# Attention scores of a decoder trunk: plain fp32 products against three products of rounded halves

## The chip, the core and the metric

The kernel runs on one core of a Trainium2 chip. The time is that of the device for one execution, in microseconds (us), and the number to be forecast is the median over several executions. PE is the matmul engine (TensorE; PEld is its weight load), DVE is VectorE, ACT is ScalarE, POOL is GpSimd, SP is the engine that issues the DMAs.

## The reference

A trunk of two layers over 256 tokens of width 1024. Layer 0 is a half-step gated FFN, a short convolution, another half-step FFN. Then one shared set of keys and values is made, and layer 1 is an FFN, sparse attention with 16 heads in 4 key groups, and an FFN. The attention has three branches over the same queries: compressed blocks of keys, selected blocks (at 256 tokens: all of them) and a window. What matters here are the three products of queries and keys:

```python
s_c = jnp.einsum('bghqd,bgnd->bghqn', qblk, k_c) * scale + head_bias(rel_c)
...
s_s = jnp.einsum('bghqd,bgqkd->bghqk', qblk, k_sel) * scale + bias_s
...
s_w = jnp.einsum('bghqd,bgkd->bghqk', qblk, k_wb) * scale + head_bias(rel_w)
```

Each is followed by a masked softmax, a product with that branch's values, and a gate; the sum of the three goes through the output weights. Everything is float32.

## The kernel before

The kernel is one long stream of matmuls. All large products are made in the type fp32r, a rounded fp32 that PE takes in one pass: a weight tile is split into a high part (a rounded copy, ACT, line 165, tile wh) and a low part (the rest, DVE, line 182, tile wl), activations likewise (xs, act), and three of the four partial products are summed. Small products, such as the scores, were left in plain fp32; the compiled program makes two matmul instructions of each.

Two places matter.

**The background of the FFN of layer 1** (`ffn_in` with `bg(f)`, f = 0 to 21, from about 500 to 625 us of the span). While PE makes the 22 column groups of the FFN, `bg(f)` is called at the end of group f and puts small steps of the key and value preparation into the engines' queues. `k_trans` (f = 6, 7) transposes the keys on PE and ACT scales them into the tile KT (tag kt). `kc_second` and `kc_norm` (f = 15, 18) make the compressed keys: a product with ones, a root on ACT, a reciprocal on DVE, and two DVE instructions that write the first 16 columns of KT. `c_values` (f = 19) makes the compressed values: POOL copies `a` into a repeated form (`a4`, line 923), and PE multiplies it (line 925).

**The attention stage** (about 700 to 760 us). Its order is written out by hand: the string `ORDER` lists words such as `S_0`, and each word calls a function that puts its instructions into the queues. Each engine executes its queue strictly in that order. The heads are handled in eight pairs j. `QT_g` (`q_trans`) transposes queries on PE into a PSUM bank; `QC_g` (`q_gain`) scales them on ACT into an act tile, which serves pairs 2g and 2g+1. `S_j` (`scores`) makes the scores of pair j in two tiles of two PSUM banks (tag mm, two of them in all): head g2 = 0 in array rows 0 to 63, g2 = 1 in rows 64 to 127, for key columns 288, 224 and 304. `M_j_g2` (`minima`, DVE) adds the bias and takes minima, which frees the PSUM tile; `E` (`exps`, ACT) makes exponentials; `R`, `N` normalise (DVE, POOL), `T`, `H` transpose (PE), `C`, `CH` copy out (ACT, or DVE with a suffix d), `U`, `V` multiply by values (PE), `O`, `P` split the result. `F` is one step of work for later on PE, the second half of the query product (`later_queries`, three matmuls a word), and `WA`, `WD` split the next weights. `GA` to `GD` make the gates. The part of the order around the first scores reads:

```python
qs_0 GT qr_0 qs_1 GC F qr_1 F root exp F F WA_0 recip qn_0 qn_1 QT_0 GA GX QC_0 F S_0 WA_1 WD_0 M_0_1 GE QT_1 M_0_0
E_0_1 E_0_0 QC_1 F F R_0_1 F S_1 F F F GD M_1_1 M_1_0 N_0_1 R_0_0 F S_2 CM_0 F F F F E_1_1 R_1_1 CX_0 N_0_0_d SQ_0
...
```

Of the kernel before, what the change touches and what calls it, by code (L numbers as in the profile page):

```python
# [9 lines left out]
F32 = mybir.dt.float32  # L10
F32R = mybir.dt.float32r
I32 = mybir.dt.int32
AF = mybir.ActivationFunctionType
ALU = mybir.AluOpType
AX = mybir.AxisListType

P = 128
T = 256
# [10 lines left out]
G_FFN1, G_MIX, G_FFN2, G_KV, G_CONV, G_Q, G_K = 0, 16, 32, 48, 56, 80, 81  # L29
# [39 lines left out]
def trunk(ctx, tc, A, out):  # L69
    nc = tc.nc  # L70
    ve, ac, pe, po, sy = nc.vector, nc.scalar, nc.tensor, nc.gpsimd, nc.sync
# [9 lines left out]
    def mk(shape, tag, bufs, dt=F32, pool=None):  # L81
        uid[0] += 1
        return (pool or sb).tile(list(shape), dt, tag=tag, name=f"{tag}_{uid[0]}", bufs=bufs)
# [3 lines left out]
    def one(shape, name, dt=F32):  # L87
        if name not in kept:
            kept[name] = cp.tile(list(shape), dt, tag=name, name=name)
        return kept[name]  # L90
# [5 lines left out]
    def bank(shape=(P, 512)):  # L96
        return mk(shape, "a", 4, pool=ps)

    def bank2():
        return mk([P, 2, 512], "mm", 2, pool=ps)  # L100

    def act(shape=(P, 512), dt=F32R):
        return mk(shape, "act", 22, dt)

    def t2(shape=(P, 512), dt=F32):
        return mk(shape, "t2", 7, dt)

    def t1(shape=(P, T)):
        return mk(shape, "t1", 6)
# [120 lines left out]
    gt = base[:, :G_N]  # L230
# [4 lines left out]
    for n, (lo, hi) in enumerate(zip(FIRST, FIRST[1:])):  # L235
# [3 lines left out]
        for dst in todo:  # L239
            m = P * dst.shape[1]  # L240
# [6 lines left out]
    parts = {(f, g): kt8[:, g[0]:g[-1] + 1, T + f * 2 * P:T + (f + 1) * 2 * P].rearrange("p k (u m) -> p u k m", u=2)  # L247
             for f in range(2) for g in GROUPS}
# [8 lines left out]
    gq = one([P, 1], "gq")  # L257
# [27 lines left out]
    def new_xs():  # L285
        return [mk([P, 512], "xs", 8, F32R) for _ in range(8)]
# [453 lines left out]


    xs = new_xs()
    xk_a = mk([P, 4, 512], "kt", 1, F32R)
    xkv = [xk_a[:, k] for k in range(4)] + [t2(dt=F32R) for _ in range(4)]
    nm = Norm([(xkv, G_KV), (xs, G_FFN1 + 8)])
    out_proj(hid, 0.5, nm)
# [72 lines left out]
    for tt in range(2):  # L819
        for x in range(2):  # L820
            src = oc[tt][:, x * 256:(x + 1) * 256].rearrange("p (a d) -> p a d", d=64)
            ac.activation(cn[tt][x], src[:, :, None, :].to_broadcast([P, 4, 2, 64]), AF.Copy, scale=rc[:, tt:tt + 1])

    KT = mk([P, 2, 528], "kt", 1)
    raw = [mk([P, 16, 64], t, NBUF) for t in ("wh", "wl")]
    for r in raw:
        po.memset(r.rearrange("p i m -> p (i m)"), 0.0)
# [2 lines left out]
    def k_trans(tt):  # L830
        pb = bank()
        for q in range(4):
            pe.transpose(pb[:, q * P:(q + 1) * P], kns[tt][:, q * P:(q + 1) * P], ident)
        for b in range(2):
            c0 = KC[b] + tt * P
            ac.activation(KT[:, :, c0:c0 + P], pb[:, b * 256:(b + 1) * 256].rearrange("p (g t) -> p g t", g=2), AF.Copy,
                          scale=gt[:, G_K + 1 + b:G_K + 2 + b])

    def c_trans(tt, x):
        pb = bank([P, 4, P])  # L840
# [65 lines left out]
    def kc_norm(pc, q):  # L906

        pb = bank()
        pe.matmul(pb[:, :64], ones, q, start=True, stop=True)
        r = t1([P, 64])  # L910
        ac.activation(r, pb[:, :64], AF.Sqrt, scale=1.0 / P, bias=epst)
        ve.reciprocal(r, r)
        for g2 in range(2):
            z = slice(g2 * 64, g2 * 64 + 64)
            v, i = [x[z, :64].rearrange("p (a g n) -> p a g n", a=2, g=2)[:, :, g2] for x in (pc, r)]
            ve.scalar_tensor_tensor(out=KT[z, :, :16], in0=v, scalar=gt[z, G_K:G_K + 1], in1=i, op0=ALU.mult, op1=ALU.mult)

    def c_values(a):

# [12 lines left out]
    def bg(f):  # L932
# [8 lines left out]
        elif f in (2, 3, 4, 5):  # L941
            c_trans((f - 2) % 2, (f - 2) // 2)
        elif f in (6, 7):
            k_trans(f - 6)
        elif f == 8:
            po.tensor_tensor(out=both, in0=ident[:, :64], in1=ident[:, 64:], op=ALU.add)
            po.tensor_tensor(out=both48, in0=ident[:96, :48], in1=ident[:96, 48:96], op=ALU.add)
        elif f == 9:
            kv["rk"] = rh_split(0)
        elif f == W1AT[0]:  # L950
            kv["ak"] = c_hidden(kv["rk"])
        elif f == 12:
            kv["ak"] = c_total(kv["ak"])
            kv["rv"] = rh_split(1)
            W.limit = NBUF
        elif f == 13:
            kv["ak"] = c_gelu(*kv["ak"])
        elif f == W1AT[1]:
            kv["av"] = c_hidden(kv["rv"])
            kv["kc"] = kc_second(kv["ak"])  # L960
        elif f == 16:
            kv["av"] = c_total(kv["av"])
        elif f == 17:
            kv["av"] = c_gelu(*kv["av"])
        elif f == 18:
            kc_norm(*kv["kc"])
        elif f == 19:
            c_values(kv["av"])
# [16 lines left out]
    qt, ct, oT, wo, wo_banks, X = {}, {}, [], [], [], {}  # L985
# [56 lines left out]
                pe.transpose(pb[:, a, tt * P:(tt + 1) * P], X["q", q, tt][:, c0 + a * P:c0 + a * P + P], ident)  # L1042

    def q_gain(g):
        q = act([P, 2, T], F32)
        ac.activation(q, X.pop(("qt", g)), AF.Copy, scale=gq)
        for a in range(2):
            qt[2 * g + a] = q[:, a]

    def later_queries():  # L1050

# [52 lines left out]
    def scores(j):  # L1104

        s = [bank2().rearrange("p a b -> p (a b)") for _ in range(2)]
        kt = KT[:, j // 4]
        k0 = kt[:, :512].rearrange("p (a b) -> p a b", a=2)[:, :, :144]
        for c0, c1, tt, k in ((0, 288, 0, k0), (288, 512, 1, kt[:, :224]), (512, 816, 1, kt[:, 224:])):
            for g2 in range(2):  # L1110
                rows = slice(g2 * 64, g2 * 64 + 64)
                pe.matmul(s[g2][:, c0:c1], qt[j][rows, tt * P:(tt + 1) * P], k[rows], start=True, stop=True)  # L1112
        X["s", j, 0], X["s", j, 1] = s

    def minima(j, g2):
# [135 lines left out]
    def wo_part(c, part):  # L1251
# [11 lines left out]
        "exp": lambda: ac.preload_act_table_set("natural_log_exp_and_others"), "qn": lambda tt: q_normed(0, tt),  # L1263
        "SQ": lambda tt: q_square(1, tt), "RD": lambda tt: q_reduce(1, tt),
        "NW": lambda: q_newton(1), "QM": lambda tt: q_normed(1, tt), "QT": q_trans, "QC": q_gain,
        "F": lambda: next(lq), "GT": g_sum, "GC": g_copy, "GA": g_total, "GX": g_trans, "GE": g_exp, "GD": g_out,
        "S": scores, "M": minima, "E": exps, "R": recip,
        "N": lambda j, g, e="": normed(j, g, ve if e else po), "T": trans, "H": trans_hi,
        "C": lambda j, g, e="": copied(("t", j, g), mk([P, 2, T], "xs", 8), copy[e]),
# [126 lines left out]
```

## Time and profile before

| what | value |
|---|---|
| median of 3 runs | 967.46 us (967.12 to 968.42) |
| span of the profiled execution | 965.5 us, 1.96 us under that median (what lies around the span) |
| PE busy | 960.8 us, 100% of the span |
| DVE busy | 730.5 us, 76% |
| ACT busy | 573.9 us, 59% |
| POOL busy | 127.8 us, 13% |
| granted PE clock | 1.000 |
| line 1112 (scores) | 96 matmul instructions, from 706.8 to 744.7 us |

The profile is one execution. Times in its views are microseconds from the start of the span. A row of the timeline gives start, duration, engine, line, operation, output and inputs, and in brackets the idle time just before it with what ended it. A row of the chain of work that ended last gives start, length and the work; there the length is the step to the next link, so a run of n matmuls divided by n is the pace at which they start. The ends of matmuls are modelled, so a PE that is busy 100% still has waits in it; the chain and the starts show them.

### The profile page before, as it was taken

The page shows a single profiled execution, that of the slowest core. Times are in us where ns is not written, and L with a number is a line of the kernel's source. Part 1 is how long each engine was busy: PE and PEld are TensorE (multiplying, and loading weights), DVE is VectorE, ACT ScalarE, POOL GpSimd, SP SyncE. Part 2 cuts the span into 40 slices and gives each one's busy share as a digit, 9 for nine tenths or more (in the row PEclk, how much of TensorE's full clock was granted, in tenths as well). Part 3 has the DMA queues.
Part 4 walks back from the last instruction along what each step waited for, and adds up shares of the span by engine and source line. Part 5 has one row for each costly group of instructions (what it writes and reads, how often), then busy time and mean ns, then how long its engine had stood idle before and what let it go on. Part 6 is the DMA issues. An engine that isn't in the chain of part 4 may idle for free.

```text
span 965.5 us, 14561 instructions
## 1 busy us (share of the span) xinstructions
PE 960.8 (100%) x5620; PEld 843.3 (87%) x5620; DVE 730.5 (76%) x1158; ACT 573.9 (59%) x977; POOL 127.8 (13%) x207
## 2 busy tenths in 40 slices
PE   9999999999999999999999999999999999999998
PEld 8888888888888888888888888888877888888888
DVE  6898875678898787865749988766579798878643
ACT  7666653555466665644656677645589776566430
POOL 2000000154420100001111012100138110000000
PEclk9999999999999999999999999999999999999999
DMA  8665554555546875545645567545511256555541
GB/s 307 215 222 183 208 177 175 202 177 198 189 170 221 234 235 179 199 159 206 217 134 173 178 218 258 174 175 191 198 57 40 93 200 236 176 182 208 183 153 60
DMA packets 28577, 177.61 MB, mean 184 GB/s; under 512 B 3115, under 2 KB 6699, under 8 KB 7900
## 3 DMA queue, kind: packets, MB, share of 16 engines
q1 hardware_dynamic: 28508, 176.69, 53.1%
q8 instruction: 44, 0.72, 0.3%
q14 instruction: 25, 0.20, 0.1%
HBM read 175.59 MB, written 1.08 MB: 183 GB/s over the span
## 4 chain that ended last, share of the span: by engine, by line
PE 96%; DVE 3%; ACT 1%; issue 0%; ACTq 0%
PE mm L425 25%; PE a L498 17%; PE mm L430 13%; PE mm L353 9%; PE a L504 9%; PE mm L358 5%; PE a L353 3%; PE a L358 2%; PE mm L1112 1%; PE mm L574 1%; PE a L761 1%; PE a L763 1%; PE a L762 1%; PE a L1189 1%; DVE wl L182 1%; PE a L1157 1%
## 5 line engine op out<-in xcount | busy, mean ns | idle before, releaser
L182 DVE TENSOR_TENSOR wl<-ws,wh 128x1024 fp32r<-128x1024 f32 x318 | 391.8, 1248 | 51.9 <-ACT wh L165 33.8
L165 ACT CAST wh<-ws 128x1024 fp32r<-128x1024 f32 x318 | 327.0, 1045 | 40.9 <-PE a L498 12.1
L425 PE MATMUL mm<-xs,wh 128*128 128x512 f32 x1088 | 255.5, 391 | 0.3 <-DVE t L368 0.3
L425 PEld LDWEIGHTS mm<-xs,wh 128*128 128x128 f32 x1088 | 201.4, 188 | 40.8 <-DVE t L368 0.8
L498 PE MATMUL a<-act,wh 128*128 128x512 f32 x714 | 167.0, 390 | 0.0
L498 PEld LDWEIGHTS a<-act,wh 128*128 128x128 f32 x714 | 132.7, 188 | 26.9
L430 PEld LDWEIGHTS mm<-xs,wl 128*128 128x128 f32 x1088 | 135.3, 191 | 2.7
L430 PE MATMUL mm<-xs,wl 128*128 128x256 f32 x1088 | 137.0, 283 | 0.0
L368 DVE TENSOR_TENSOR t<-mm,t 128x512 f32<-128x512 f32 x95 | 65.4, 688 | 68.7 <-ACT t L367 67.8
L367 ACT COPY t<-mm 128x512 f32<-128x512 f32 x95 | 55.7, 586 | 95.3 <-PE mm L430 49.2
L353 PE MATMUL mm<-xs,wh 128*128 128x512 f32 x400 | 96.9, 392 | 0.0
L504 PEld LDWEIGHTS a<-act,wl 128*128 128x128 f32 x714 | 89.0, 192 | 1.8
L504 PE MATMUL a<-act,wl 128*128 128x256 f32 x714 | 89.9, 283 | 0.0
L353 PEld LDWEIGHTS mm<-xs,wh 128*128 128x128 f32 x400 | 73.3, 188 | 13.9
L314 POOL TENSOR_TENSOR sq<-sq,t 128x256 f32<-128x256 f32 x35 | 27.7, 791 | 388.6 <-ACT t L312 388.5
L457 DVE SCALAR_TENSOR_TENSOR base<-a,base 128x256 f32<-128x256 f32 x78 | 32.9, 422 | 56.6 <-PE a L498 54.3
L384 ACT ACTIVATE t<-t 128x256 f32<-128x256 f32 x88 | 36.8, 418 | 62.3 <-DVE t L372 62.2
L297 ACT ACTIVATE xs<-base 128x256 fp32r<-128x256 f32 x48 | 24.0, 505 | 78.7 <-DVE base L457 69.7
L372 DVE TENSOR_TENSOR t<-t,R 128x512 f32<-128x512 f32 x88 | 61.6, 700 | 2.6
L361 ACT CAST act<-t 128x256 fp32r<-128x256 f32 x96 | 39.1, 407 | 29.8 <-DVE t L690 19.3
L358 PEld LDWEIGHTS mm<-xs,wl 128*128 128x128 f32 x400 | 52.1, 191 | 2.4
L358 PE MATMUL mm<-xs,wl 128*128 128x256 f32 x400 | 52.9, 283 | 0.0
(267 smaller groups left out, 917.2 us busy)
## 6 DMA issues: line engine op xcount, KB each, us to landing
ws<-in_ffn_w_in_dram SPq DMA_DIRECT2D x85, 1024.0 KB, 4.9
ws<-in_ffn_w_out_dram SPq DMA_DIRECT2D x44, 1024.0 KB, 4.8
ws<-in_conv_w_in_dram SPq DMA_DIRECT2D x12, 1024.0 KB, 4.8
ws<-in_w_kv_dram SPq DMA_DIRECT2D x6, 1024.0 KB, 5.2
ws<-in_conv_w_out_dram SPq DMA_DIRECT2D x4, 1024.0 KB, 4.9
ws<-in_attn_w_q_dram SPq DMA_DIRECT2D x4, 1024.0 KB, 4.9
ws<-in_attn_w_o_dram SPq DMA_DIRECT2D x4, 1024.0 KB, 4.8
base<-row_d SPq DMA_DIRECT2D x8, 256.0 KB, 6.3
```

Of the source, the lines that this page charges most:

```text
L165: ac.copy(h, src)
L182: ve.tensor_tensor(out=l, in0=src, in1=h.bitcast(F32), op=ALU.subtract)
L353: pe.matmul(o, u[0][:, k * P:(k + 1) * P], xs[k], start=(k == 0), stop=False)
L358: pe.matmul(o[:, :T], u[1][:, k * P:(k + 1) * P], xs[k][:, :T], start=False, stop=(k == last))
L361: ac.copy(dst[:, :T], src)
L367: ac.copy(r, o[:, :, T:])
L368: ve.tensor_tensor(out=r, in0=o[:, :, :T], in1=r, op=ALU.add)
L372: ve.tensor_tensor(out=r, in0=r, in1=R[:, None, :].to_broadcast([P, n, T]), op=ALU.mult)
L425: pe.matmul(o[:, x], us[x][0][:, k * P:(k + 1) * P], xs[k], start=(k == 0), stop=(k == last))
L430: pe.matmul(o[:, x, :T], us[x][1][:, k * P:(k + 1) * P], xs[k][:, :T], start=False, stop=(k == last))
L498: pe.matmul(o, run[k][0], lhs[k], start=(k == 0), stop=(k == last))
L504: pe.matmul(o[:, :T], run[k][1], lhs[k][:, :T], start=False, stop=(k == last))
```

## The change

Keys and queries are kept as rounded high parts and remaining low parts, and each score is the sum of three fp32r products (high with high, low query with high key, high query with low key), still in the two row halves.

```diff
-    xk_a = mk([P, 4, 512], "kt", 1, F32R)
+    xk_a = mk([P, 2112], "kt", 1, F32R)[:, :2048].rearrange("p (k n) -> p k n", k=4)
...
-    KT = mk([P, 2, 528], "kt", 1)
+    KT = mk([P, 2112], "kt", 1, F32R).rearrange("p (x a n) -> p x a n", x=2, a=2)
...
     def k_trans(tt):
...
-            ac.activation(KT[:, :, c0:c0 + P], pb[:, b * 256:(b + 1) * 256].rearrange("p (g t) -> p g t", g=2), AF.Copy,
-                          scale=gt[:, G_K + 1 + b:G_K + 2 + b])
+            src, g = pb[:, b * 256:(b + 1) * 256].rearrange("p (g t) -> p g t", g=2), gt[:, G_K + 1 + b:G_K + 2 + b]
+            hi, lo = [KT[:, x, :, c0:c0 + P] for x in range(2)]
+            ac.activation(hi, src, AF.Copy, scale=g)
+            ve.scalar_tensor_tensor(out=lo, in0=src, scalar=g, in1=hi.bitcast(F32), op0=ALU.mult, op1=ALU.subtract)
...
     def kc_norm(pc, q):
...
+        kc = t1([P, 2, 16])
         for g2 in range(2):
             z = slice(g2 * 64, g2 * 64 + 64)
             v, i = [x[z, :64].rearrange("p (a g n) -> p a g n", a=2, g=2)[:, :, g2] for x in (pc, r)]
-            ve.scalar_tensor_tensor(out=KT[z, :, :16], in0=v, scalar=gt[z, G_K:G_K + 1], in1=i, op0=ALU.mult, op1=ALU.mult)
+            ve.scalar_tensor_tensor(out=kc[z], in0=v, scalar=gt[z, G_K:G_K + 1], in1=i, op0=ALU.mult, op1=ALU.mult)
+        hi, lo = [KT[:, x, :, :16] for x in range(2)]
+        ac.copy(hi, kc)
+        po.tensor_tensor(out=lo, in0=kc, in1=hi.bitcast(F32), op=ALU.subtract)
...
     def q_gain(g):
-        q = act([P, 2, T], F32)
-        ac.activation(q, X.pop(("qt", g)), AF.Copy, scale=gq)
+        pb, hi, lo = X.pop(("qt", g)), act([P, 2, T]), act([P, 2, T])
+        ac.activation(hi, pb, AF.Copy, scale=gq)
+        ve.scalar_tensor_tensor(out=lo, in0=pb, scalar=gq, in1=hi.bitcast(F32), op0=ALU.mult, op1=ALU.subtract)
         for a in range(2):
-            qt[2 * g + a] = q[:, a]
+            qt[2 * g + a] = hi[:, a], lo[:, a]
...
     def scores(j):
...
-        for c0, c1, tt, k in ((0, 288, 0, k0), (288, 512, 1, kt[:, :224]), (512, 816, 1, kt[:, 224:])):
-            for g2 in range(2):
-                rows = slice(g2 * 64, g2 * 64 + 64)
-                pe.matmul(s[g2][:, c0:c1], qt[j][rows, tt * P:(tt + 1) * P], k[rows], start=True, stop=True)
+        parts = []
+        for x in range(2):
+            kt = KT[:, x, j // 4]
+            parts.append((kt[:, :512].rearrange("p (a b) -> p a b", a=2)[:, :, :144], kt[:, :224], kt[:, 224:]))
+        for n, (c0, c1, tt) in enumerate(((0, 288, 0), (288, 512, 1), (512, 816, 1))):
+            for m, (a, b) in enumerate(((0, 0), (1, 0), (0, 1))):
+                for g2 in range(2):
+                    rows = slice(g2 * 64, g2 * 64 + 64)
+                    pe.matmul(s[g2][:, c0:c1], qt[j][a][rows, tt * P:(tt + 1) * P], parts[b][n][rows], start=(m == 0), stop=(m == 2))
```

The string `ORDER` stays as it is. The words that now issue more are `QC` (one DVE instruction more) and `S` (18 matmuls instead of 6 in the program), and in the background `k_trans` (two DVE instructions more a call) and `kc_norm` (one ACT and one POOL instruction more). Where these land in the queues is shown at three places. Line numbers of the changed kernel are up to 10 higher.

The first place is POOL's queue at the end of the FFN's background. In it, L891 and L892 (L893 and L894 after) finish the GELU of the compressed values, L923 (L929 after) is the copy a4 of `c_values`, and L314 belongs to the norm that follows the FFN. Before:

```order
L886 TENSOR_TENSOR t_1019_5933<-t_1019_5933,t_1018_5932 128x64
L891 TENSOR_SCALAR t_1019_5933<-t_1019_5933 128x64
L892 TENSOR_TENSOR t_1018_5932<-t_1018_5932,t_1019_5933 128x64
L923 COPY t_1050_6106<-t_1018_5932 128x256
L314 TENSOR_TENSOR sq_6230<-sq_6230,t_1093_6355 128x256
```

The same place after the change:

```order
L888 TENSOR_TENSOR t_1019_5937<-t_1019_5937,t_1018_5936 128x64
L893 TENSOR_SCALAR t_1019_5937<-t_1019_5937 128x64
L894 TENSOR_TENSOR t_1018_5936<-t_1018_5936,t_1019_5937 128x64
L922 TENSOR_TENSOR kt_4849<-t_1040_6056,kt_4849 128x2x16
L929 COPY t_1051_6113<-t_1018_5936 128x256
L314 TENSOR_TENSOR sq_6237<-sq_6237,t_1094_6362 128x256
```

The low part of the compressed keys (L922) now stands ahead of the copy that `c_values` needs.

The second place is DVE's queue from the end of the first pair's minima to the start of the second pair's. The ISA rows are the instructions of `M` (an operation and the read of its accumulator); L1124 is the compressed part of `M`, L1135 is `R_0_1`, L1094 to L1096 are `GD`. Before:

```order
L1120 ISA pr_6915,sm_6916<-base,mm_6886 128x256
L1120 ISA sm_6916 128x1
L1124 TENSOR_TENSOR t_1178_6906<-cbias,mm_6886 128x2x16
L1135 RECIPROCAL sm_6922<-sm_6922 128x4
L1094 TENSOR_SCALAR G<-G 128x96
L1095 RECIPROCAL G<-G 128x96
L1096 TENSOR_SCALAR G<-G,small 128x16
L1120 ISA pr_6965,sm_6966<-base,mm_6945 128x128
```

The same place after the change, with the names' line numbers 7 to 10 higher:

```order
L1130 ISA pr_6936,sm_6937<-base,mm_6895 128x256
L1130 ISA sm_6937 128x1
L1134 TENSOR_TENSOR t_1180_6927<-cbias,mm_6895 128x2x16
L1053 SCALAR_TENSOR_TENSOR act_6954<-a_6931,gq,act_6953 128x512
L1145 RECIPROCAL sm_6943<-sm_6943 128x4
L1101 TENSOR_SCALAR G<-G 128x96
L1102 RECIPROCAL G<-G 128x96
L1103 TENSOR_SCALAR G<-G,small 128x16
L1130 ISA pr_7000,sm_7001<-base,mm_6968 128x128
```

The low part of the second group of queries (L1053, from `QC_1`) now stands between the first pair's minima and everything that follows. It reads the high part that ACT writes, and in ACT's queue that instruction stands behind the eight exponentials of the first pair:

```order
L1052 ACTIVATE act_6888<-a_6877,gq 128x512
L165 CAST wh_6915<-ws_6779 128x1024
L1097 ACTIVATE G<-a_6883,sm_6886 128x48 x2
L1141 ACTIVATE pr_6921,sm_6943<-pr_6921,sm_6922 128x128 x2
L1141 ACTIVATE pr_6921,sm_6943<-pr_6921,sm_6922 128x256 x2
L1141 ACTIVATE pr_6936,sm_6948<-pr_6936,sm_6937 128x128 x2
L1141 ACTIVATE pr_6936,sm_6948<-pr_6936,sm_6937 128x256 x2
L1052 ACTIVATE act_6953<-a_6931,gq 128x512
L1141 ACTIVATE pr_7000,sm_7057<-pr_7000,sm_7001 128x128 x2
```

This is ACT's order after the change; it is the same as before but for numbers, so the second L1052 was there too, and only PE read its result.

More of the change, by code (lines that the diff above doesn't have):

```diff
@@ L1106, in scores @@
         s = [bank2().rearrange("p a b -> p (a b)") for _ in range(2)]
-        kt = KT[:, j // 4]
-        k0 = kt[:, :512].rearrange("p (a b) -> p a b", a=2)[:, :, :144]
-        for c0, c1, tt, k in ((0, 288, 0, k0), (288, 512, 1, kt[:, :224]), (512, 816, 1, kt[:, 224:])):
-            for g2 in range(2):
-                rows = slice(g2 * 64, g2 * 64 + 64)
-                pe.matmul(s[g2][:, c0:c1], qt[j][rows, tt * P:(tt + 1) * P], k[rows], start=True, stop=True)
+        parts = []
[7 more added lines that the diff above has]
+                    pe.matmul(s[g2][:, c0:c1], qt[j][a][rows, tt * P:(tt + 1) * P], parts[b][n][rows], start=(m == 0), stop=(m == 2))
         X["s", j, 0], X["s", j, 1] = s
```

## The prediction

> **What bounds the kernel now.** I read the page first: the shares of the engines and the chain of work that ended last.
>
> ```profile
> span 965.5 us, 14561 instructions
> PE 960.8 (100%) x5620; PEld 843.3 (87%) x5620; DVE 730.5 (76%) x1158; ACT 573.9 (59%) x977; POOL 127.8 (13%) x207
> PE 96%; DVE 3%; ACT 1%; issue 0%; ACTq 0%
> ```
>
> PE bounds the whole: the chain runs through it for 96% of the span. A stall of PE inside an FFN is therefore lost, unless a later wait gives it back, and work saved on PE counts only where PE is not about to wait for someone. For that the average says nothing, so I read the busy time by stretches of the attention stage.
>
> ```profile
> 710.00:720.00 10.00, 10.00 (x53) 7.21 (x53) 9.20 (x57) 9.23 (x39) 6.24 (x16) 1.00 0.01 3
> 720.00:730.00 10.00, 9.62 (x81) 7.31 (x79) 8.82 (x46) 9.65 (x33) 6.38 (x17) 1.00 0.01 2
> 730.00:740.00 10.00, 10.00 (x92) 7.85 (x89) 9.30 (x57) 9.92 (x40) 8.17 (x20) 1.00 0.00 1
> 740.00:750.00 10.00, 10.00 (x86) 7.99 (x85) 9.87 (x45) 9.57 (x39) 8.01 (x17) 1.00 0.33 107
> ```
>
> The columns are PE, PEld, DVE, ACT, POOL. Here DVE is busy 37.2 of 40 us and ACT 38.4. Three engines are full at once, each in a fixed order. PE has little to win here by itself, and a delay of DVE or ACT has almost nowhere to go.
>
> **The change part by part. First, the scores on PE.** The paces come from the chain (length over count) and one timeline row.
>
> ```profile
> 544.67 4.13 PE mm L425 x18
> 548.80 3.83 PE mm L430 x32
> 706.91 1.58 PE mm L1112 x12
> 734.55 0.86 PE a L1189 x8
> 735.41 0.44 PE a L1193 x8
> 706.84 0.51 PE L1112 MATMUL mm<-kt,act 64*128 64x288 f32 x2
> ```
>
> An fp32r matmul of 512 columns takes 0.229 us (L425), one of 256 takes 0.120 (L430): 0.43 ns a column and 0.01 us beside. Plain fp32 in array halves (L1189, L1193: two column halves at once, so four pairs a row) takes 0.215 us a pair for 256 columns, 0.84 ns a column. The last row, asked for the first 0.06 us of a score, shows that both row halves start together. So the old score is six pairs over 2 x 816 columns, 1632 x 0.84 = 1.37 us, and 0.2 of entry: the 1.58 measured. The new one is nine pairs over 3 x 816 columns, 2448 x 0.43 + 9 x 0.01 = 1.14 us. Saved: 0.24 us a score, 1.9 for eight; by the column price alone (no fixed part) at most 0.34 and 2.7. That weight loads keep this pace is read from L430: a load for every 0.120 us, and L1193 issues two loads and two matmuls every 0.11.
>
> Each new pair loads fresh weights into the half that the pair before is using. The Trainium skill ("TensorE: Matmul & The Clock Gate", section "Part 3: Packing small matmuls — row/col tiling") says that a weight load overlaps running matmuls only when their row groups differ. By that a load would stand between any two pairs, and nine would cost about 2 us; but L430 loads all rows for each matmul and still takes 0.120 us, so the trace disagrees for the whole array and no row shows it for fp32r in halves.
>
> **Second, the compressed keys and POOL's queue.** This is the largest term, and it is not in the scores.
>
> ```profile
> 610.70 0.40 POOL L923 COPY t<-t 128x256 f32<-128x256 f32 x1
> 616.58 0.31 ACT L911 ACTIVATE t<-a,epst 128x64 f32<-128x64 f32 x1
> 617.51 0.52 DVE L916 SCALAR_TENSOR_TENSOR kt<-a,base,t 64x32 f32<-64x32 f32 x2
> 618.06 0.69 DVE L368 TENSOR_TENSOR t<-mm,t 128x512 f32<-128x512 f32 x1
> 616.46 0.55 PE L925 MATMUL a<-small,t 128*128 128x64 f32 x4
> 617.01 4.18 PE mm L425 x18
> ```
>
> Before, POOL makes the copy a4 (L923) at 610.70, as soon as its input is there, and PE uses it at 616.46 without a wait. Now POOL's queue holds the low part of the compressed keys ahead of that copy. The low part needs ACT's rounded copy, which needs the two DVE instructions L916, and these end at 618.03. From there: the ACT copy of 128x32 (nearest row L911, 128x64, 0.31; I take 0.3), the POOL subtraction (nearest L923, 256 columns, 0.40; I take 0.3), the copy a4 (0.40), and four hand-overs of 0.03 to 0.1 (DVE to DVE here 0.03): PE can start L925 at about 619.2. It stalls 2.7 us; 2.4 if the new steps take 0.2 each, 3.2 if they take half a microsecond each. Queued behind L925 is the next column group of the FFN (the x18 row), so nothing fills the gap. Behind the ACT copy stands the next group's evacuation, late by 1.5 us, while PE is late by more.
>
> **Third, the keys' low parts in `k_trans`.** In the changed program ACT's second scaling of a call waits for DVE's first low part, so the two alternate.
>
> ```profile
> 545.70 0.42 DVE L362 TENSOR_TENSOR act<-t,act 128x256 fp32r<-128x256 f32 x1
> 545.67 0.59 ACT L367 COPY t<-mm 128x512 f32<-128x512 f32 x1
> 546.29 0.69 DVE L368 TENSOR_TENSOR t<-mm,t 128x512 f32<-128x512 f32 x1 [0.17 <-ACT t L367]
> L301 DVE SCALAR_TENSOR_TENSOR xs<-base,xs 128x256 fp32r<-128x256 f32 x3 | 1.4, 480 | 0.6 <-ACT xs L297 0.6
> L1031 DVE TENSOR_TENSOR t<-a,sm 128x512 f32<-128x512 f32 x2 | 1.3, 686 | 0.0
> ```
>
> After L362 come a low part (0.48, as L301), ACT's second scaling (0.42), then L367 and L368: L368 ends at 548.2 instead of 546.98. It frees the bank that PE takes for the last two of the x18 row at 544.67, that is 16 x 0.229 later, at 548.3. Hidden with 0.1 us to spare; I take 0.1 of cost, and 0 to 0.6 as bounds. If that cover were gone, PE would wait for L368.
>
> **Fourth, the queries' low parts in the attention stage.** Each is 128x512 from PSUM, priced as L1031: 0.69, the next starting some 0.04 to 0.08 earlier, so 0.65.
>
> ```profile
> 708.53 0.29 DVE L1120 CUSTOM_DVE_ANT_0 pr<-base,mm 128x128 f32<-128x128 f32 x1 [1.69 <-PE mm L1112]
> 710.93 0.17 DVE L1135 RECIPROCAL sm<-sm 128x4 f32<-128x4 f32 x1
> 712.76 0.29 DVE L1120 CUSTOM_DVE_ANT_0 pr<-base,mm 128x128 f32<-128x128 f32 x1 [0.50 <-PE mm L1112]
> 712.39 0.67 ACT L1046 ACTIVATE act<-a,gq 128x512 f32<-128x512 f32 x1
> 713.09 0.40 ACT L1131 ACTIVATE pr<-pr,sm 128x128 f32<-128x128 f32 x1
> 717.23 0.18 DVE L1135 RECIPROCAL sm<-sm 128x4 f32<-128x4 f32 x1 [0.17 <-ACT pr L1131]
> 722.49 0.17 DVE L1022 SCALAR_TENSOR_TENSOR sm<-sm 128x16 f32<-128x16 f32 x1 [0.67 <-ACT sm L1020]
> 727.70 0.68 DVE L1167 COPY xs<-a 128x512 f32<-128x512 f32 x1
> 728.69 0.18 DVE L1135 RECIPROCAL sm<-sm 128x4 f32<-128x4 f32 x1 [0.31 <-ACT pr L1131]
> 728.55 0.68 ACT L1046 ACTIVATE act<-a,gq 128x512 f32<-128x512 f32 x1
> 733.04 0.29 DVE L1120 CUSTOM_DVE_ANT_0 pr<-base,mm 128x128 f32<-128x128 f32 x1 [0.60 <-PE mm L1112]
> ```
>
> `QC_0`: DVE waits 1.69 us for the first score, and the low part fits in; PE's first score waits for it about 0.1 and is shorter by 0.24. Nothing.
>
> `QC_1`: DVE is ready for its low part at 710.93. ACT writes the high part from 712.39 to 713.06, behind the first pair's exponentials. DVE stands still 2.16 us, then works 0.65; behind it wait `R_0_1`, the gates and `M_1_1`. Of these 2.81 us the idle 0.50 before `M_1_1` is given back: `M_1_1` comes 2.3 late, and so does its exponential on ACT at 713.09, which waited for nothing else. The second score cannot help: its tile was long ready.
>
> `QC_2`: 0.65 of DVE work, its high part being there in time. `QC_3`: it stands ahead of the copy at 727.70, and its high part is ready at 729.23, 1.5 later; DVE is by then later than ACT by one low part, so I take a wait of 0.8, and 0.65 of work. In all DVE is 2.3 + 0.65 + 0.8 + 0.65 = 4.4 us late. The waits it had after 713 (0.17, 0.67, 0.31, 0.60, together 1.75) can give back that much; from 733 to 749 it had none. I take 2.7, with 1.0 (PE, which has steps to fill with, tolerates another 1.7) and 4.4 (nothing given back) as ends. The 1.9 us saved on PE fall into its waits for `M` to free the score tiles and for copies, and are not counted again.
>
> **The sum.** 2.7 + 0.1 + 2.7 = +5.5 us on the span of 965.5, so 971.0. The median of the runs stands 1.96 above that span, which gives 967.46 + 5.5 = 973.0. With the ends of the terms, +3.4 to +8.2: 970.9 to 975.7.
>
> **The rivals.**
>
> *PE paces the attention stage (not slower).* The chain goes through PE nearly all the way there; if the steps behind `QC_1` have 2.3 us of slack before PE needs them, the late DVE costs nothing and the scores' saving of 1.9 to 2.7 us counts: 967.46 + 2.8 - 1.9 to 2.7 = 967.6 to 968.4. It decides at whether `M_1_1`, 2.3 late, holds up the third score, whose tiles it frees. Against it: DVE at 9.2 and 8.8 of 10 in the stretches that would have to take up the delay.
>
> *The halves don't run at once in fp32r.* Then a score is 18 matmuls of about 0.127 (0.11 to 0.13 by width), 2.3 us instead of 1.14. DVE waits for scores and scores for DVE in turn, so between none and all of 8 x 1.15 = 9.2 shows; I take half, 4.5: 977.5. For it: no row shows such a pair. Against it: plain fp32 pairs do start together. The load rule above would give nearly the same.
>
> *The stall lowers PE's rate.* At the start PE runs slowly for some microseconds after idling:
>
> ```profile
> 4.56 2.03 PE L574 MATMUL mm<-xs,wh 128*128 128x256 f32 x8
> 7.61 1.12 PE L574 MATMUL mm<-xs,wh 128*128 128x256 f32 x8
> ```
>
> The same eight matmuls take 0.25 us each at first and 0.14 later. If 2.7 us of idleness brought that back for as long as at the start (1.05 to about 6.4 us), it would cost up to 2.5 us more: 975.5. The Trainium skill ("TensorE: Matmul & The Clock Gate", section "Why this matters for your kernels") advises against PE-idle gaps over about 3 us, since an idle window halves the clock; the stall forecast here lies just under that, and no stall of this size is in the trace before.
>
> **How the numbers follow.** The forecast as worked out: 0.67. PE paces: 0.10. Halves one after the other: 0.13. Slow PE after the stall: 0.07. Something else: 0.03. The range 970.2 to 977.0 leaves out the first rival and the upper part of the second. A change under 0.2% (965.5 to 969.4) is about what a measurement of this kernel cannot tell from none. Slower by more: 0.67 + 0.13 + 0.07 and part of the rest, 0.88; within: 0.09, nearly all from the first rival; faster: 0.03.
>
> **What would show it.** Right: PE idle for 2.4 to 3.2 us before the compressed values' product, released by POOL; DVE idle about 2 us before the second low part of the queries, released by ACT; a score of 1.2 to 1.4 us in the chain. Wrong: no POOL wait there, or a third score that starts as early after the second as before, or scores over 2 us.

## The result, and the profile after

The changed kernel took 976.52 us (median of 5 runs, 974.51 to 977.45), the kernel before 967.12 (5 runs, 966.69 to 968.42): a ratio of 1.0088 [1.0077, 1.0099], slower. The profiled execution took 974.73 us with a span of 972.9. The page of the changed kernel, its span, its engines and its chain of work, answering to the first lines shown of before:

```profile
span 972.9 us, 14666 instructions
PE 962.2 (99%) x5668; PEld 844.9 (87%) x5668; DVE 735.4 (76%) x1166; ACT 574.1 (59%) x978; POOL 127.1 (13%) x208
PE 91%; DVE 4%; ACT 2%; issue 1%; DMA 1%; POOL 0%; SPq 0%; POOLq 0%; ACTq 0%
```

PE carries 91% of the chain instead of 96. What it lost shows in two places (0.2 us more in a third, `k_trans`, further down). The first is the product of `c_values` and the way to it. The rows are timeline rows of the changed kernel: start, length, engine, line, what it does, and in brackets the idle time before it with its releaser.

```profile
617.68 0.51 DVE L919 SCALAR_TENSOR_TENSOR t<-a,base,t 64x32 f32<-64x32 f32 x2
618.23 0.22 ACT L921 CAST kt<-t 128x32 fp32r<-128x32 f32 x1 [1.24 <-DVE t L919]
618.52 0.25 POOL L922 TENSOR_TENSOR kt<-t,kt 128x32 fp32r<-128x32 f32 x1 [7.79 <-ACT kt L921]
618.72 0.40 POOL L929 COPY t<-t 128x256 f32<-128x256 f32 x1
619.17 1.02 PE L931 MATMUL a<-small,t 128*128 128x64 f32 x4 [2.45 <-POOL t L929]
```

POOL stands idle for 7.79 us until ACT's rounded copy is there, and the copy a4 (L929), which was made at 610.70 before, comes at 618.72. PE is idle for 2.45 us. But the product itself then takes 1.02 us where it took 0.55, so I read the next rows of the chain and the granted clock (PEclk, the third column from the right) in steps of 1 us:

```profile
619.17 1.02 PE a L931 x4
620.18 5.44 PE mm L425 x18
625.62 3.83 PE mm L430 x32
```

```profile
619.00:620.00 1.00, 0.83 (x5) 0.83 (x5) 0.97 (x2) 0.88 (x1) 0.11 (x1) 0.65 0.97 410
620.00:621.00 1.00, 1.00 (x4) 0.81 (x4) 1.00 (x2) 0.54 (x1) 0.00 (x0) 0.50 0.09 25
621.00:622.00 1.00, 1.00 (x4) 0.81 (x3) 0.52 (x1) 0.99 (x2) 0.00 (x0) 0.50 0.00 0
622.00:623.00 1.00, 1.00 (x4) 0.76 (x4) 0.43 (x1) 1.00 (x2) 0.00 (x0) 0.64 0.00 0
```

From about 619.3 to 622.7 the clock is granted at 0.50, and at 1.00 in the rows just before and after these four. The losses of these rows are 0.35 + 0.50 + 0.50 + 0.36 = 1.71 us, and the 18 products take 5.44 us instead of 4.18. The product of `c_values` and those 18 together are 1.7 us longer than before (1.01 + 5.44 against 0.55 + 4.18, each up to the next start), so the whole difference there is the clock.

The second place is the attention stage. The rows of DVE's low part for groups 0, 1 and 3 (that of group 2, at 733.48, waits for nothing) and the first row of `M_1_1`, then those of the first three scores on PE:

```profile
710.96 0.75 DVE L1053 SCALAR_TENSOR_TENSOR act<-a,gq,act 128x512 fp32r<-128x512 f32 x1 [1.36 <-ACT act L1052]
717.65 0.75 DVE L1053 SCALAR_TENSOR_TENSOR act<-a,gq,act 128x512 fp32r<-128x512 f32 x1 [2.08 <-ACT act L1052]
719.55 0.28 DVE L1130 CUSTOM_DVE_ANT_0 pr<-base,mm 128x128 f32<-128x128 f32 x1
735.56 0.75 DVE L1053 SCALAR_TENSOR_TENSOR act<-a,gq,act 128x512 fp32r<-128x512 f32 x1 [0.67 <-ACT act L1052]
```

```profile
711.27 1.77 PE L1122 MATMUL mm<-kt,act 64*128 64x288 f32 x18
715.64 1.42 PE L1122 MATMUL mm<-kt,act 64*128 64x288 f32 x18
720.98 0.37 PE L1122 MATMUL mm<-kt,act 64*128 64x288 f32 x1 [0.97 <-DVE t L1134]
722.08 1.43 PE L1122 MATMUL mm<-kt,act 64*128 64x288 f32 x17 [0.74 <-DVE t L1134]
```

The second low part waits 2.08 us for the high part that stands behind ACT's exponentials. `M_1_1` (L1130, behind the gates) starts at 719.55, with no wait of its own, and the third score stands on PE for 0.97 and again 0.74 us until `M` (L1134) frees its tiles. The third score's seventeen further products begin 10.81 us after the first score's start, where before the whole score began 8.75 after it (715.59 after 706.84): 2.1 later.

To place the loss in every kernel below I use four marks of PE, all of them starts, counted from its first matmul: the first product of `c_values`, the first score, the last product of the last score, and the last matmul. "Falls" are stretches with the clock at 0.50 inside the kernel; excesses are against before, in us. The first column also holds what varies at the program's start: without a POOL wait it moves by 0.3 to 0.4 either way, and over four profiles of the changed kernel itself from 2.21 to 2.80. Every kernel with the change has 0.2 us of `k_trans` in it too, shown further down.

| profiled execution | us | first `c_values` | from there to the first score | the scores | the rest | falls |
|---|---|---|---|---|---|---|
| before | 967.46 | 615.40 | 90.38 | 37.42 | 218.09 | 0 |
| the changed kernel | 974.73 | +2.71 | +1.73 | +3.03 | -0.01 | 1 |
| the changed kernel again (e10, first) | 974.12 | +2.21 | +1.69 | +3.00 | -0.04 | 1 |
| the changed kernel again (e10, second) | 976.12 | +2.61 | +1.70 | +4.54 | 0.00 | 2 |
| the changed kernel again (e10, third) | 973.22 | +2.80 | +0.11 | +3.03 | 0.00 | 0 |
| low part of the compressed keys behind a4 (e1) | 972.24 | +0.38 | 0.00 | +4.55 | +0.03 | 1 |
| low parts of the queries later (e2) | 974.48 | +3.47 | +3.11 | +0.62 | 0.00 | 1, twice as long |
| both (e3) | 968.04 | +0.14 | +0.01 | +0.61 | +0.01 | 0 |
| POOL wait filled on PE (e4) | 973.39 | +3.01 | +0.09 | +3.00 | +0.01 | 0 |
| no low parts of the queries (e5) | 965.98 | -0.29 | +0.01 | -0.98 | -0.02 | 0 |
| before, with one POOL copy (e6) | 970.93 | +2.07 | +1.60 | +0.01 | 0.00 | 1 |
| before, with six (e8) | 974.34 | +5.37 | +1.69 | +0.01 | 0.00 | 1 |

### The profile page after: what moved, and what is told of

Read it like the earlier page. It is cut to its first block, busy times and chain, and to the rows that moved or that the text cites. A ratio compares the mean times of both kernels' runs of the same rounds, so it can differ in the third digit from the quotient of the medians.

```text
span 972.9 us, 14666 instructions
## 1 busy us (share of the span) xinstructions
PE 962.2 (99%) x5668; PEld 844.9 (87%) x5668; DVE 735.4 (76%) x1166; ACT 574.1 (59%) x978; POOL 127.1 (13%) x208
## 4 chain that ended last, share of the span: by engine, by line
PE 91%; DVE 4%; ACT 2%; issue 1%; DMA 1%; POOL 0%; SPq 0%; POOLq 0%; ACTq 0%
PE mm L425 24%; PE a L498 17%; PE mm L430 13%; PE mm L353 9%; PE a L504 9%; PE mm L358 5%; PE a L353 3%; PE a L358 2%; PE a L761 1%; PE a L763 1%; PE a L762 1%; ACT pr L1141 1%; PE mm L574 1%; DVE wl L182 1%; PE a L1199 1%
## 5 line engine op out<-in xcount | busy, mean ns | idle before, releaser
L368 DVE TENSOR_TENSOR t<-mm,t 128x512 f32<-128x512 f32 x95 | 65.4, 688 | 69.3 <-ACT t L367 68.4
L314 POOL TENSOR_TENSOR sq<-sq,t 128x256 f32<-128x256 f32 x35 | 27.6, 789 | 385.3 <-ACT t L312 385.1
```

What stands on the lines that cost most here:

```text
L368: ve.tensor_tensor(out=r, in0=o[:, :, :T], in1=r, op=ALU.add)
```

## The experiments

The theory after the result: two waits, one for each instruction that stands ahead of something urgent in an in-order queue (the sum as forecast), and on top of them a clock that falls after a wait. The rivals: that the slow rows are part of the new work (the new instructions, or memory that they share), that the clock follows something else than the wait, or that the attention stage is slower because three rounded products simply don't pay.

The runs of e1 to e4 stand beside 17 runs of the kernel before with a median of 967.01, those of e5, e6 and e8 beside 16 with 967.16.

**e1: the low part of the compressed keys behind the copy a4.** Only the place in POOL's queue changes.

```diff
 def kc_norm(pc, q):
...
-        po.tensor_tensor(out=lo, in0=kc, in1=hi.bitcast(F32), op=ALU.subtract)
+        kv["low"] = lambda: po.tensor_tensor(out=lo, in0=kc, in1=hi.bitcast(F32), op=ALU.subtract)
...
         elif f == 19:
             c_values(kv["av"])
+            kv["low"]()
```

> The changed kernel with one instruction moved: POOL's subtraction for the low part of the compressed keys is issued after the copy a4 that the compressed values' product waits for. Theory (the order in POOL's queue made PE stand 2.45 us, and that idleness made PE slow for the 5 us after it, 1.9 us more): both go, PE starts that product without a wait, the granted clock is 1.000 throughout, and only the attention stage's loss of about 2.6 to 2.9 is left: 969.9 to 970.4 against 967.1 before. Rival (the stall only moves: ACT's copy still makes the next evacuation 1.5 us late, and PE then waits for a PSUM tile): 972 to 974, with a PE wait for DVE line 368 within 10 us.

972.62 us (5 runs, 970.25 to 972.90), ratio 1.0051 [1.0039, 1.0063]. The product of `c_values` runs at once and at full pace:

```profile
616.83 0.55 PE L931 MATMUL a<-small,t 128*128 128x64 f32 x4
617.20 4.37 PE L425 MATMUL mm<-xs,wh 128*128 128x512 f32 x18
```

So the POOL wait is gone, and the slow rows behind it. But the profiled run has a new one, behind the waits of the third score. Its windows, the third score, and the first of the later query products (`F`) behind it (0.79 us where such a product takes 0.39 elsewhere):

```profile
715.00:720.00 5.00, 3.27 (x24) 2.29 (x23) 4.71 (x29) 4.17 (x18) 3.63 (x10) 0.93 0.01 2
720.00:725.00 5.00, 4.83 (x20) 3.70 (x18) 3.83 (x23) 3.00 (x12) 3.77 (x9) 0.73 0.00 2
```

```profile
716.93 0.37 PE L1123 MATMUL mm<-kt,act 64*128 64x288 f32 x1 [0.98 <-DVE t L1135]
718.04 1.47 PE L1123 MATMUL mm<-kt,act 64*128 64x288 f32 x17 [0.74 <-DVE t L1135]
719.44 0.79 PE L1067 MATMUL a<-wh,xs 128*128 128x512 f32 x1
```

Loss by the windows: 0.07 x 5 + 0.27 x 5 = 1.70 us, the same amount as behind the POOL wait. Four of its five runs have a mean granted clock of 0.998; the one with 1.000 took 970.25, as the theory had it. The median lies 2.4 us above that, of which a fall is 1.7, and so in the range that was named for the rival. But the rival's mechanism is not there: from the product of `c_values` to the first score the kernel takes as long as before. What the theory missed is that the second wait can bring a fall as well.

**e2: the low parts of the queries later.** `QL`, the DVE half of `QC`, becomes a step of its own. In the order it stands right behind `QC` for groups 0 and 2, behind `M_1_1` for group 1 and behind `M_4_0` for group 3. POOL's queue is that of the changed kernel.

```diff
-E_0_1 E_0_0 QC_1 F F R_0_1 F S_1 F F F GD M_1_1 M_1_0 ...
+E_0_1 E_0_0 QC_1 F F R_0_1 F S_1 F F F GD M_1_1 QL_1 M_1_0 ...
...
+    def q_low(g):
+        pb, hi, lo = X.pop(("qt", g)), X.pop(("qh", g)), act([P, 2, T])
         ve.scalar_tensor_tensor(out=lo, in0=pb, scalar=gq, in1=hi.bitcast(F32), op0=ALU.mult, op1=ALU.subtract)
```

> The changed kernel with the low part of the queries as a word of its own, two of the four placed later in DVE's order (the second group's after the second pair's first minima, the fourth's after the fifth pair's first minima); POOL's order as in the changed kernel. Theory (it is DVE's wait behind ACT, not its added work, that costs the attention stage): 2.6 less than the changed kernel, 972.1 if the granted clock is as in its profiled run, up to 974 with the lower clock of its other runs; DVE no longer waits 2 us for ACT line 1052. Rival (the four instructions' 2.8 us of work costs it, in a stage where DVE is full): at most 0.5 less, 974.2 or more.

972.15 us (6 runs, 970.45 to 974.48), ratio 1.0051 [1.0037, 1.0065]. The excess within the scores drops from 3.03 to 0.62: DVE's waits for ACT at `QC_1` and `QC_3` made 2.4 us of the stage's loss; the products and DVE's added work leave the 0.62. The edit moves both low parts and doesn't part them; in the changed kernel the fourth score starts 1.86 us late, counted from the first, and the last one 3.14, so `QC_1` has the larger share. The POOL wait is untouched, and its fall was twice as long in the profiled run (18 products in 6.96 us):

```profile
619.93 1.12 PE L931 MATMUL a<-small,t 128*128 128x64 f32 x4 [2.45 <-POOL t L929]
620.81 6.96 PE L425 MATMUL mm<-xs,wh 128*128 128x512 f32 x18
```

The three runs with a clock of 1.000 took 970.45 to 970.91; those with 0.996 to 0.998 took 973.39 to 974.48. So the median stands in a gap between two groups, and that it meets the 972.1 of the theory is chance. Without a fall on either side the edit brings 2.3 to 2.8 us (973.22 against 970.45 to 970.91), where the theory had 2.6.

**e3: both edits together.** If the two waits are all there is, next to nothing stays.

> Both moves together. If the two losses are separate and each is one of order: nothing of the FFN's loss and nearly nothing of the attention stage's is left, 967.1 to 967.7, the same as before within 0.2%, although each score is 0.24 us shorter. If the scores' saving counts once the order is right (PE paces the stage): 965.2 to 965.6. If DVE's added work costs: 969 or more.

968.67 us (11 runs, 967.32 to 971.27), ratio 1.0015 [1.0006, 1.0024]. None of the three ranges holds it; it lies between the first and the third. The profile, of a run of 968.04, places 0.6 us within the scores and 0.2 in `k_trans`. The medians differ by 1.66 us, more than that; of the other 0.8 no profile shows the place, and it stays open.

**e4: the POOL wait filled on PE.** The changed kernel, with 12 plain products of ones (64 columns) issued ahead of the waiting product. PE comes to the product as late as in the changed kernel, but not idle. Each is two matmul instructions in the trace; the product that follows overwrites their sums.

```diff
+            for _ in range(12 if q == 0 else 0):
+                pe.matmul(pc[:, 0], ones, ones[:, :64], start=True, stop=True)
             pe.matmul(pc[:, q], a4[:, 2 * q:2 * q + 2].rearrange("p g x n -> p (g x n)"), w2[1], start=True, stop=True)
```

> The changed kernel with twelve small plain fp32 products (ones with ones, 64 columns, results overwritten) put on PE just ahead of the compressed values' product, about 2.4 us of work in the stall. Theory (idleness slows PE afterwards): the stall stays as long as it was, but the matmuls behind it run at full pace (18 in 4.2 us instead of 5.4) and the granted clock is 1.000: 1.9 less than the changed kernel's fastest runs, 972.6 to 973.0, and its spread of 3 us is gone. Rival (the slow matmuls come from something else at that place, late weights or operands): no faster than the changed kernel, 974.5 or more.

973.24 us (5 runs, 972.39 to 975.66), ratio 1.0065 [1.0053, 1.0077]: 3.3 us faster than the changed kernel, with 12 more products in it, and 0.2 above the range of the theory. The 18 products are back at full pace, and the clock at 1.00:

```profile
616.84 2.79 PE L932 MATMUL a<-ones 128*128 128x64 f32 x24
619.47 0.65 PE L933 MATMUL a<-small,t 128*128 128x64 f32 x4
619.92 4.36 PE L425 MATMUL mm<-xs,wh 128*128 128x512 f32 x18
```

```profile
620.00:625.00 5.00, 5.00 (x28) 4.26 (x27) 3.79 (x5) 3.52 (x7) 0.00 (x0) 1.00 0.06 23
```

POOL and ACT do the same work as late as in the changed kernel, and PE comes to the product as late; only its idleness is gone. Four of the five runs had a clock of 1.000. So it is the idleness, not the new work, that the fall follows. The one profile would not show that, since a profile of the changed kernel can be without a fall too (e10); the four runs do, and e6 and e8, where the fall comes with none of the new work. The spread did not go, as had been expected: one run, with a clock of 0.998, took 975.66. The edit can take away one fall of 1.7 us only, the one behind the POOL wait; why the third score's waits, which stay, brought one fall at most in five runs, these runs don't show. The other four show about what the two waits cost by themselves.

**e5: no low parts of the queries.** e1's order, and the query's high part stands in for its low part. The scores so lack the product of the keys' high part and the queries' low part; the count of matmuls is the same, DVE has four instructions less.

```diff
-        pb, hi, lo = X.pop(("qt", g)), act([P, 2, T]), act([P, 2, T])
+        pb, hi = X.pop(("qt", g)), act([P, 2, T])
+        lo = hi
         ac.activation(hi, pb, AF.Copy, scale=gq)
-        ve.scalar_tensor_tensor(out=lo, in0=pb, scalar=gq, in1=hi.bitcast(F32), op0=ALU.mult, op1=ALU.subtract)
```

> The changed kernel with POOL's subtraction after the copy a4, and without the low part of the queries: DVE's four instructions are left out and the high part stands in their place in the second product, so all 144 score matmuls run but the scores lack the queries' low part. It has the shorter scores without DVE's added work and waits. If DVE and ACT pace the attention stage: from first to last score 36.4 to 37.4 us against 37.42 before, 966.0 to 967.3 in all. If PE paces it, the whole 1.9 shows: 35.5 us, 965.1 or less. If the 0.6 us that the stage still loses with both moves comes from something other than DVE's four instructions: 38 us, 967.7 or more.

966.40 us (11 runs, 965.98 to 967.28), ratio 0.9991 [0.9982, 1.0000]. The shorter scores, with nothing to pay for on DVE, bring 0.98 us within the scores, about half of the 1.9 that the products save. Against e3, the four low parts cost 0.98 + 0.62 = 1.6 us even at good places. It is as forecast for a stage that DVE and ACT pace (36.44 us from first to last score, 36.4 to 37.4 expected). In the middle of the stage ACT is full:

```profile
720.00:730.00 10.00, 9.55 (x95) 7.80 (x94) 9.02 (x49) 9.88 (x36) 6.48 (x17) 1.00 0.01 2
730.00:740.00 10.00, 9.89 (x103) 7.74 (x103) 9.38 (x49) 10.00 (x41) 7.88 (x20) 1.00 0.01 3
```

ACT, the fourth pair, is busy 19.9 of these 20 us, and its exponentials hold 16.3% of the chain between 700 and 765 us, the largest share. That the other half of the saving falls into waits, for ACT above all, follows from this; it was not tried on a kernel with a lighter ACT.

**e6 and e8: the kernel before, with one and with six POOL copies ahead of a4.** Nothing of the change but a wait: a copy of the 32 compressed columns of `KT` into a tile that nobody reads. It is what POOL's subtraction waits for, without any rounding. e6 has one such copy, e8 six.

```diff
             ve.scalar_tensor_tensor(out=KT[z, :, :16], in0=v, scalar=gt[z, G_K:G_K + 1], in1=i, op0=ALU.mult, op1=ALU.mult)
+        for _ in range(6):
+            po.tensor_copy(out=t1([P, 2, 16]), in_=KT[:, :, :16])
```

> The kernel before with one POOL instruction added: a copy of the compressed keys' 32 columns into an unused tile, issued where the change has its subtraction, so POOL waits for DVE's two instructions ahead of the copy a4; nothing else changes. Theory (order in POOL's queue alone makes the stall): PE idle 2.0 to 2.2 us before the compressed values' product, +2.3 in runs whose granted clock stays at 1.000 (969.3), and 1.5 to 3 more in those where it falls (971 to 972); attention stage as before, 37.4 us from first to last score. Rival (the stall needs ACT's rounded copy or the added work in the keys): no change, 967.

> The same with six such copies, so that PE's idle time grows by about 1 us to 3.1 to 3.4. If the lower clock follows from the length of the idle time: the granted clock is below 1.000 in all runs, 970.5 plus 2 to 3, 972.5 to 973.5. If it is chance whatever the length: some runs at 1.000 and 970.5, as with one copy.

e6: 970.96 us (6 runs, 969.64 to 971.22), ratio 1.0034 [1.0022, 1.0047]. e8: 974.41 (5 runs, 974.27 to 975.84), ratio 1.0078 [1.0065, 1.0090]. In e6 one 32-column copy, which no result needs, makes this kernel 3.8 us slower:

```profile
618.53 1.11 PE L926 MATMUL a<-small,t 128*128 128x64 f32 x4 [2.14 <-POOL t L924]
619.40 5.46 PE L425 MATMUL mm<-xs,wh 128*128 128x512 f32 x18
```

And in e8:

```profile
621.83 0.79 PE L927 MATMUL a<-small,t 128*128 128x64 f32 x4 [4.35 <-POOL t L925]
622.37 5.88 PE L425 MATMUL mm<-xs,wh 128*128 128x512 f32 x18
```

PE idles for 2.14 and for 4.35 us, and the stretch that follows, up to the first score, is 1.60 and 1.69 us longer: in these two, one fall costs the same after twice the wait. e6 came out as forecast; in e8 all five runs had a clock below 1.000, as the theory of length had it, but the five further copies added 2.2 us of idle time, not 1, so the time lies above its range.

**e10: the changed kernel, three more profiles.** The longer runs of the changed kernel, 976.5 to 977.5 us, have a granted clock of 0.996 to 0.997. e1 had shown that the third score's waits can bring a fall, e2 that one fall can last twice as long; either would do.

> The changed kernel unaltered, looked at once more to see where a longer run of it loses its clock. Its first profile (974.7 us, granted clock 0.998) had one fall, after the wait for POOL; the runs of 976.5 to 977.5 have 0.996 to 0.997. Theory of two falls: in a profile of such a run the clock is below 1 both at 620 to 625 us and at about 720 us, where the attention stage waits for M_1_1, each costing 1.3 to 2 us. Rival, one fall that lasts longer: below 1 only after the wait for POOL, the row of 18 products there at about 7 us instead of 5.4, and 1.00 from 715 to 730. If the run is of 974 to 975 us it tells nothing of this.

> The same as the look before it: two falls give a clock below 1 at 620 to 625 us and again at about 720 us in a run of 976 us or more; one longer fall gives 1.00 from 715 to 730 and a row of 18 products of about 7 us after the wait for POOL.

> The same as the two looks before it: two falls give a clock below 1 at 620 to 625 us and again at about 720 us in a run of 976 us or more; one longer fall gives 1.00 from 715 to 730 and a row of 18 products of about 7 us after the wait for POOL.

They took 974.12, 976.12 and 973.22 us beside 966.51 for before, with clocks of 0.998, 0.996 and 1.000. The first has one fall, at 620, as the first profile had. The second has two; its windows at both places (the second fall runs over a border):

```profile
620.00:625.00 5.00, 5.00 (x17) 3.92 (x16) 3.68 (x6) 3.42 (x7) 0.00 (x0) 0.66 0.05 18
720.00:725.00 5.00, 3.41 (x22) 2.63 (x23) 4.73 (x30) 4.77 (x22) 4.19 (x10) 0.80 0.00 2
725.00:730.00 5.00, 4.62 (x26) 3.75 (x24) 3.34 (x18) 3.21 (x12) 2.84 (x9) 0.85 0.01 2
```

0.34 x 5 = 1.70 us at the first, (0.20 + 0.15) x 5 = 1.75 at the second. The third has none, behind the same wait:

```profile
619.26 0.66 PE L931 MATMUL a<-small,t 128*128 128x64 f32 x4 [2.45 <-POOL t L929]
619.73 4.37 PE L425 MATMUL mm<-xs,wh 128*128 128x512 f32 x18
```

So the theory of two falls holds for this run: none, one and two falls gave 973.2, 974.1 and 976.1 us. The first and the third differ by 0.9 and not by 1.7 because the first column of the table differs by 0.6 the other way. That each of the longer runs without a profile had two falls, and not one of twice the length, is not shown: their times of 976.5 to 977.5 would fit either, and a mean clock of 0.996 doesn't count falls, since e8 took 974.27 with 0.996 and 974.34 with 0.998.

## Why the prediction was right, and where its size was off

The mechanism was right: two waits, each at the place and with the releaser that was named, and a saving on PE that doesn't show. The forecast of 973.0 is within 0.3 us of the one run of the changed kernel without a fall (973.22). That is closer than the terms deserve: by that run's marks the excess is 5.9 us, against 5.5 forecast. That the median of 976.52 lies within the range is luck. The terms' own ends went up to 975.7; the range went on to 977.0 for the rival of halves one after the other, which did not happen. Term by term:

- **The second term, POOL's queue, +2.7 forecast.** Idle 2.45 us, the product 2.71 later. The steps were shorter than taken (ACT's copy 0.22 and POOL's subtraction 0.25, each taken as 0.3), but all of it lay 0.2 to 0.3 us later in the span, and so PE started at 619.17 against 619.2. e1 takes it away, e6 makes it in the kernel before.
- **The third term, `k_trans`, +0.1 forecast.** About 0.2. DVE waits 0.54 us for ACT's second scaling, and L368 ends at 548.1. The row of 18 products that needs its bank takes 4.33 us where it took 4.13 before (544.67 to 548.80): its last two products start 0.1 us late each. So the cover was just gone and PE waited, within the bounds given (0 to 0.6). The same delay stands in all nine profiles with the change and in none without it:

```profile
546.95 0.48 DVE L839 SCALAR_TENSOR_TENSOR kt<-a,base,kt 128x256 fp32r<-128x256 f32 x1 [0.54 <-ACT kt L838]
547.42 0.69 DVE L368 TENSOR_TENSOR t<-mm,t 128x512 f32<-128x512 f32 x1
544.57 4.33 PE mm L425 x18
```

- **The fourth term, the queries' low parts, +2.7 forecast.** +3.03 in the scores. DVE waited 2.08 us at `QC_1` (2.16 forecast) and 0.67 at `QC_3` (0.8); a low part took 0.75 us, not 0.69. The decision point named for the first rival, whether `M_1_1` holds up the third score, went as the forecast had it. `QC_0` was forecast to cost nothing: the first score took 1.77 us where it took 1.65 before and the second one 1.42, so PE waited 0.35 in it, not 0.1, and 0.1 is lost.
- **The first term, the scores on PE, 1.9 saved and not counted.** The chain's last score (the one before it takes the same):

```profile
750.67 1.35 PE mm L1122 x18
```

  1.35 instead of 1.58: 0.23 each, 0.24 forecast. (The bound given beside it, 0.34, comes to 0.32 by the column prices it names.) The saving is real and mostly unused, as forecast, in the changed kernel; e5 shows that about 1 us of it can be had when DVE has nothing to pay.
- **The rival of halves one after the other (0.13).** Refuted by the same rows: 2.3 us a score would have been seen. The Trainium skill ("TensorE: Matmul & The Clock Gate", section "Part 3: Packing small matmuls — row/col tiling") says that a weight load overlaps running matmuls only when the row groups differ; by the prediction's estimate that would make about 2 us of nine pairs. With 1.35, entry included, the trace does not agree for fp32r in halves.
- **The step that failed: the sum held no term for the clock.** The rival that the stall lowers PE's rate had a chance of 0.07, and it took place in the changed kernel's first profile and in two of the three that followed. It had been given up to 2.5 us, from the slow matmuls at the program's start. That row is the clock: the trace's records of the granted clock, of which PEclk is the mean, begin with full speed at 6.45 us in the profile of the kernel before and at 3.98 us in e6's, and in each of the twelve profiles the matmuls come to their full pace at that moment. The products of ones and the eight behind them are the same instructions in both; first a row of before, then two of e6:

```profile
3.77 1.06 PE L253 MATMUL a<-ones 128*128 128x128 f32 x4
3.77 0.71 PE L253 MATMUL a<-ones 128*128 128x128 f32 x4
4.49 1.19 PE L574 MATMUL mm<-xs,wh 128*128 128x256 f32 x8
```

  The eight took 2.03 us in the kernel before. (The windows of the profile count time ahead of the first record as 1.00.) But the slow stretch at the start, 5.4 us long, is longer than a fall inside the kernel, 3.4 us. So the price of one fall was set too high and its chance too low, and that there can be two was not seen.

  The fall costs 1.7 us a time, and it may come behind the POOL wait, behind the third score's waits, or both. 967.46 + 2.7 + 3.0 and two falls of 1.7 make 976.6, which is the median within 0.1; for those runs the two falls are inferred. The Trainium skill (same page, section "Why this matters for your kernels") sets the point at PE-idle gaps over about 3 us; here 2.14 and 2.45 us were enough in most profiles, and so in e1 were two waits of 0.98 and 0.74 with a single product between. Reading that sentence as a threshold that a stall of 2.4 to 2.7 would stay under is the one ground that the prediction gives for a small chance, beside the lack of such a stall in the trace before.

## What to carry to other kernels

An instruction that is cheap on an idle engine is priced by what it waits for and by what is queued behind it: 0.25 us of POOL work cost 2.5 us here, and issued behind the urgent copy it cost nothing that a profile shows. Where a full PE is made to wait for about 1.7 us or more, in one piece or in two close together, add a possible fall of the clock to the wait, and look at the granted clock in steps of 1 us before blaming the code behind it. Work saved on PE in a stage where DVE and ACT are full pays only if it asks nothing of them, and even then only in part (1.0 of 1.9 us in e5).

## What the runs showed of the hardware

The fall has a size. In each profile that has one, the clock is granted at 0.50 for 3.41 us (1.71 us lost in the changed kernel's 1-us windows), whether PE had idled 2.14, 2.45 or 4.35 us; in e2 it lasted twice that, with 3.1 us lost. It is not certain to come: behind the same wait of 2.45 us it came in four profiles (the changed kernel, two of its three repeats, e2) and not in one.

The traces show what goes with it. Between its first rise, 3.98 to 6.92 us into the span, and its last change, the clock is recorded at full or half in stretches that are all whole numbers of one step of 3.413 us (614.40, 713.39 and 959.14 us at full speed are 180, 209 and 281 steps, a fall is one, that of e2 two). So a wait counts by how much of it lies within one step. Here are the steps around the POOL wait in the changed kernel, then in its third repeat, which has no fall, and around the third score in its second repeat. The second figure is the step's length, the third PE's busy time:

```profile
615.89:619.30 3.41, 0.96 (x5) 0.50 (x4) 1.94 (x6) 2.16 (x5) 0.59 (x2) 1.00 0.66 223
619.30:622.71 3.41, 3.41 (x11) 2.83 (x12) 2.61 (x4) 2.81 (x4) 0.00 (x0) 0.50 0.22 89
614.49:617.90 3.41, 2.32 (x11) 1.58 (x9) 2.72 (x6) 2.45 (x4) 0.00 (x0) 1.00 0.25 43
617.90:621.32 3.42, 2.06 (x11) 1.80 (x12) 2.60 (x5) 2.42 (x4) 0.59 (x2) 1.00 0.65 268
719.62:723.04 3.42, 1.71 (x19) 1.27 (x18) 3.38 (x25) 3.29 (x14) 2.56 (x7) 1.00 0.01 2
723.04:726.45 3.41, 3.41 (x12) 2.52 (x9) 3.14 (x18) 2.87 (x13) 3.33 (x8) 0.50 0.01 2
```

In the first, all 2.45 us of the wait lie in one step, and the next step is slow. In the second, the end of a step cuts the same wait into 1.09 and 1.36 us, and none is. Each of the eight falls inside these kernels follows a step in which PE idled 1.71 to 3.02 us; the longest idle time in a step without one is 1.48 us. This is read off twelve profiles; no run moved a wait against the steps, and the bound is not sharp: at the very end of e2, where the program's work runs out, a step with 1.30 us idle was followed by a slow one. Why e2's fall held for a second step is open too; 0.38 us of the wait still lay in its first one, against 0.14 in e6, where it did not.

The falls make the same program end at 973.2, 974.1 or 976.1 us, so a spread of runs can itself be a sign of a wait on PE.

fp32r products run in the two row halves at once with fresh weights for each: eighteen in 1.35 us, where eighteen one after the other, at the 0.127 that the prediction works out, would take 2.3.
